# Three of seven products of an Up job keep adding in a bank that another product has filled, and each weight tile is fetched by itself

## The chip, the core and the metric

The kernel runs on one core of a Trainium2 chip. Its engines work side by side: TensorE multiplies matrices and leaves the result in PSUM banks, VectorE and ScalarE work element by element, GpSimd has little to do here, and SyncE issues DMA transfers. Each engine takes its instructions in order. The metric is the time of the whole program in microseconds of the device: median 3076.38 us of 3 runs (3075.09 to 3080.23).

## What is computed

A trunk of two layers over 16 learned tokens and a sequence of 1024, 1040 tokens of width 1024 in float32. Layer 0 mixes tokens by a gated delta rule, layer 1 by an mLSTM. Each is followed by the same MLP, which is where the change lies:

```
def squared_relu_mlp(h, w_up, w_down):
    a = jax.nn.relu(h @ w_up)
    return (a * a) @ w_down

for layer in range(2):
    h = h + mixer(rms_norm(h, attn_norm[layer]))
    h = h + squared_relu_mlp(rms_norm(h, ffn_norm[layer]), ff_up[layer], ff_down[layer])
```

`w_up` is 1024 x 4096, `w_down` 4096 x 1024.

## The kernel before

Everything that is multiplied is split into a high and a low part, and one product is three matmuls (`mm3`, lines 115 to 118): high by high, high by low, low by high.

**Up.** `Up` (line 1025) multiplies by a Strassen-Winograd scheme of two by two blocks: seven products of half size stand for eight. A job is one pair of 128-column strips of `w_up`; there are 16 pairs. Its two weight tiles are r1 (`wraw`, a ring of two buffers) and r2 (one buffer), 512 KB each, which `load` fetches together. `operand` makes the seven weight operands from them: up to four subtractions of 128x512 on VectorE (line 1055), and for each operand a cast on ScalarE (the high part, line 1071) and a subtraction on VectorE (the low part, line 1072). An operand is made three products ahead of its use, in one of four buffers.

The tokens are taken in two halves. A product is twelve matmuls of 128x260 a half (128x256 in layer 1, which leaves the learned tokens out). A job for one half has seven products of twelve matmuls, a job for both has seven of twenty-four. Each layer runs 21 jobs: three for the first half only, while `Norm.combine` (in the background) still makes the operands xhi and xlo of the second half on VectorE and ScalarE; then eleven for both halves, with five one-half jobs between them; and two for one half at the end, at the first of which `first_done` begins to load and split the activation tiles a_st for `Down`.

**Evacuation.** A product's sum stands in one of three PSUM buffers of two banks (`pu`), taken in turn, so a product can begin when the one three before it has been read. `evac` (line 1075) builds the four results with running sums: u is a copy of a11's product (ScalarE), c = u + a12, u = u + s2, v = u + s3, c = v + s1, u = u + s1, c = v + a22, c = u + s4. Those are seven VectorE additions a job. Each c then passes relu and square on ScalarE and goes to the tensor `acts` (d_a) in DRAM.

The program's text gives what depends on what; a scheduler then fixes the order on each engine from its own estimate of times.

Of the kernel before, what the change touches and what calls it, by code (L numbers as in the profile page):

```python
# [7 lines left out]
F32 = mybir.dt.float32  # L8
F32R = mybir.dt.float32r
AF = mybir.ActivationFunctionType  # L10
ALU = mybir.AluOpType
AX = mybir.AxisListType
PSUM = bass.MemoryType.PSUM
DRAM = bass.MemoryType.DRAM

P = 128
D = 1024
KT = D // P
# [37 lines left out]
class Ctx:  # L56
    def __init__(self, tc, stack):
        self.tc = tc
        self.nc = tc.nc
        self.stack = stack  # L60
        self.bg = []
        self.wx = None
# [49 lines left out]

def mm3(nc, ps, whi, wlo, xhi, xlo, first, last):
    nc.tensor.matmul(ps, whi, xhi, start=first, stop=False)  # L116
    nc.tensor.matmul(ps, whi, xlo, start=False, stop=False)  # L117
    nc.tensor.matmul(ps, wlo, xhi, start=False, stop=last)  # L118


def staging(c, shape):
    n = 1
    for d in shape[1:]:
        n *= d
    raw = c.wraw.tile([P, 2 * HALF], F32, tag="wraw", name="wraw")[:, :n]
    return raw.rearrange("p (a b) -> p a b", a=shape[1]) if len(shape) == 3 else raw
# [13 lines left out]
def rows_view(w):  # L140
    return w.rearrange("(k p) f -> p k f", p=P)
# [63 lines left out]
class GDN:  # L205
# [239 lines left out]
    def dense(self, whl, hf, g, m=P):  # L445
        c, n = self.c, GL[hf] // 2
        ps = c.pj.tile([P, 512], F32, tag="pj", name="ps_in")[:m, :n]
        gs = slice(g * n, (g + 1) * n)
        for k in range(KT):
            xhi, xlo = self.xh[k // 2]  # L450
            mm3(self.nc, ps, whl[0][:, k], whl[1][:, k], xhi[:, k % 2, gs], xlo[:, k % 2, gs], k == 0, k == KT - 1)
            if k == KT // 2 - 1:
                yield
        return ps, gs
# [391 lines left out]
class OutUnits:  # L846
# [20 lines left out]
    def unit(self, hf, k8, add, before=None):  # L867
        c, nc = self.c, self.nc
        x = self.pre
        at = self.order.index((hf, k8))  # L870
        w0 = self.load_w(k8, 0)
        x += [self.heads(hf, 4 * k8 + j, at == 3) for j in range(len(x), 4)]
        self.pre = []
        for d in range(KT):
            if before:
                before(d)
            whi, wlo = self.load_w(k8, d) if d else w0
            for g in range(2):
                gs = slice(g * G, (g + 1) * G)
                ps = c.pj.tile([P, 512], F32, tag="pj", name="ps_out")[:, :G]  # L880
                for h in range(8):
                    hi, lo = (t[:, h % 2, gs] for t in x[h // 2])
                    mm3(nc, ps, whi[:, h], wlo[:, h], hi, lo, h == 0, h == 7)
                    if h % 4 == 3:
                        yield
                add(d, g, ps)
            if d == 5 and at < 3:
                nhf, nk8 = self.order[at + 1]
                self.pre = [self.heads(nhf, 4 * nk8 + j, at == 1 and j > 0) for j in range((1, 3, 3)[at])]
# [137 lines left out]
class Up:  # L1027

    ORDER = (("a11", 0), ("a12", 1), ("s2", 4), ("s3", 5), ("s1", 3), ("a22", 6), ("s4", 2))

    def __init__(self, c, w_up, norm, acts, stack, side):
        self.c, self.nc, self.w, self.norm, self.acts = c, c.nc, w_up, norm, acts
        self.u1 = c.pool("u1", 1, stack, side=side)
        self.u3 = c.pool("u3", 3, stack, side=side)
        self.ps = c.pool("pu", 3, stack, space=PSUM)
        self.nop = 0

    def load(self, i):  # L1040
        nc, c, w = self.nc, self.c, rows_view(self.w)
        r1 = staging(c, [P, KT, P])
        nc.sync.dma_start(out=r1, in_=w[:, :, 2 * i * P:(2 * i + 1) * P])
        r2 = self.u1.tile([P, KT, P], F32, tag="r2", name="r2")
        nc.sync.dma_start(out=r2, in_=w[:, :, (2 * i + 1) * P:(2 * i + 2) * P])
        return r1, r2

    def operand(self, raw, name):

# [25 lines left out]
    def evac(self, i, hs, name, ps, tmp):  # L1075

        nc = self.nc

        def tile(pool, n):
            return pool.tile([P, 2, self.norm.g], F32, tag=n, name="up_" + n)[:, hs]  # L1080

        def add(out, x):
            nc.vector.tensor_tensor(out, x, ps, op=ALU.add)  # L1083

        def finish(s, t, x):
            out = tile(self.u3, "c")
            add(out, x)
            nc.scalar.activation(out, out, AF.Relu)
            nc.scalar.activation(out, out, AF.Square)
            nc.scalar.dma_start(out=self.acts[i][:, s, hs, t], in_=out)  # L1090
        if name == "a11":
            tmp["u"] = tile(self.u1, "u")
            nc.scalar.copy(tmp["u"], ps)
        elif name == "a12":
            finish(0, 0, tmp["u"])
        elif name == "s2":
            add(tmp["u"], tmp["u"])
        elif name == "s3":
            tmp["v"] = tile(self.u1, "v")
            add(tmp["v"], tmp["u"])  # L1100
        elif name == "s1":
            finish(1, 1, tmp["v"])
            add(tmp["u"], tmp["u"])
        elif name == "a22":
            finish(1, 0, tmp["v"])
        else:
            finish(0, 1, tmp["u"])

    def run(self, jobs):

        n, ahead = len(self.ORDER), 3
        raws, ops = {0: list(self.load(jobs[0][0]))}, {}
        done = 0
        for ji, (i, parts, before) in enumerate(jobs):
            if before:
                before()
            hs = slice(parts[0], parts[-1] + 1)
            tmp = {}
            for u, (name, xi) in enumerate(self.ORDER):
                while done <= min(ji * n + u + ahead, len(jobs) * n - 1):  # L1120
                    dj, du = divmod(done, n)
                    ops[done] = self.operand(raws[dj], self.ORDER[du][0])
                    if du == n - 1 and dj + 1 < len(jobs):
                        raws[dj + 1] = list(self.load(jobs[dj + 1][0]))
                    done += 1
                w = ops.pop(ji * n + u)
                ps = self.ps.tile([P, 2, 512], F32, tag="pu", name="ps_up")[:, :, :self.norm.g]
                for hf in parts:
                    for k in range(4):
                        hi, lo = (x[:, xi] for x in self.norm.x[hf][k])  # L1130
                        mm3(self.nc, ps[:, hf], w[:, k], w[:, 4 + k], hi, lo, k == 0, k == 3)
                    yield
                self.evac(i, hs, name, ps[:, hs], tmp)

# [599 lines left out]
```

## Time and profile before

| | us |
|---|---|
| median of 3 runs | 3076.38 (3075.09 to 3080.23) |
| profiled execution, device time | 3077.17 |
| its span, first to last instruction | 3075.5 |
| TensorE busy | 3002.4 (98%) |
| VectorE busy | 1934.5 (63%) |
| ScalarE busy | 1473.1 (48%) |
| Up of layer 0 in the span | about 1163 to 1522 |
| Up of layer 1 in the span | about 2369 to 2706 |

Busy times are sums over one profiled execution. "Idle before" names how long an engine stood before an instruction and what released it. The granted clock is TensorE's, in parts of its full 2.4 GHz; 0.5 is the lower of its two levels, 1.2 GHz. A matmul's duration is modelled from its start to its end in a pipeline, so the time of a row of matmuls is read from their starts.

### The profile page before, as it was taken

The numbers are of one execution on the slowest core, as the hardware profiler recorded it, in microseconds if no ns is written. First come the engines' busy times: TensorE is split into PE (matmuls) and PEld (weight loads), VectorE is DVE, ScalarE is ACT, GpSimd is POOL, SyncE is SP. The second block draws the span as 40 slices with busy tenths as digits, with TensorE's granted clock in tenths as the row PEclk, the third lists the DMA queues.
The fourth block names the chain that finished last, engine by engine and source line by source line (L and its number), as shares of the span: only waits on it lengthen the run. The fifth ranks groups of instructions, "written<-read, shape, count | busy, mean of one in ns | idle before, by whom it ended". The sixth has DMA issues, their size and how long they took to land.

```text
span 3075.5 us, 63578 instructions
## 1 busy us (share of the span) xinstructions
PE 3002.4 (98%) x25836; PEld 2848.9 (93%) x25836; DVE 1934.5 (63%) x4393; ACT 1473.1 (48%) x3358; POOL 301.8 (10%) x534
## 2 busy tenths in 40 slices
PE   7999999999999998999999999999999899999999
PEld 7999999999999897999999999999998899988887
DVE  6867777777776568775644547234468876654443
ACT  5666766766664445555411114444444565531112
POOL 1333332232221000000000000000000000000000
PEclk9999999999999999999999999999999999999999
DMA  4333233333234733443423312222132443342223
GB/s 108 82 84 91 83 88 95 86 89 100 81 91 146 237 110 93 138 125 105 155 76 98 104 63 80 66 65 63 61 95 85 122 127 114 115 149 79 93 89 103
DMA packets 401892, 310.22 MB, mean 101 GB/s; under 512 B 29855, under 2 KB 366112, under 8 KB 401600
## 3 DMA queue, kind: packets, MB, share of 16 engines
q1 hardware_dynamic: 366000, 272.32, 30.2%
q10 hardware_dynamic: 35600, 33.84, 3.2%
q8 instruction: 204, 3.34, 0.5%
q14 instruction: 88, 0.72, 0.1%
HBM read 247.79 MB, written 58.31 MB: 100 GB/s over the span
## 4 chain that ended last, share of the span: by engine, by line
PE 84%; DVE 8%; DMA 4%; ACT 2%; POOL 1%; issue 1%; SPq 0%; DVEq 0%; ACTq 0%; POOLq 0%
PE ps_dn L118 8%; PE ps_dn L117 8%; PE ps_dn L116 8%; PE ps_up L116 6%; PE ps_up L117 6%; PE ps_up L118 6%; PE ps_in L118 5%; PE ps_in L116 5%; PE ps_in L117 5%; PE ps_m L116 3%; PE ps_m L117 3%; PE ps_m L118 3%; PE ps_out L116 2%; PE ps_out L117 2%; PE ps_out L118 2%
## 5 line engine op out<-in xcount | busy, mean ns | idle before, releaser
L116 PE MATMUL ps_up<-xhi,uop 128*128 128x260 f32 (+1 forms) x1792 | 509.1, 285 | 21.6 <-DVE up_u L1083 7.1
L118 PE MATMUL ps_up<-xhi,uop 128*128 128x260 f32 (+1 forms) x1792 | 506.5, 283 | 5.1 <-DVE uop L1072 5.1
L117 PE MATMUL ps_up<-xlo,uop 128*128 128x260 f32 (+1 forms) x1792 | 507.6, 283 | 0.7 <-DVE xlo L1020 0.7
L135 ACT CAST whi<-wraw 128x1024 fp32r<-128x1024 f32 (+1 forms) x248 | 255.8, 1032 | 503.8 <-PE ps_dn L117 359.9
L118 PE MATMUL ps_dn<-act_hi,wlo 128*128 128x260 f32 (+1 forms) x1536 | 492.8, 321 | 0.0
L117 PE MATMUL ps_dn<-act_lo,whi 128*128 128x260 f32 (+1 forms) x1536 | 492.3, 320 | 0.0
L116 PE MATMUL ps_dn<-act_hi,whi 128*128 128x260 f32 (+1 forms) x1536 | 490.4, 319 | 0.8 <-DVE up_c L1083 0.7
L116 PE MATMUL ps_in<-act_hi,whi 128*128 128x264 f32 (+1 forms) x1536 | 451.6, 294 | 2.6 <-ACT sz L526 1.7
L118 PE MATMUL ps_in<-act_hi,wlo 128*128 128x264 f32 (+1 forms) x1536 | 448.8, 292 | 0.0
L117 PE MATMUL ps_in<-act_lo,whi 128*128 128x264 f32 (+1 forms) x1536 | 446.6, 291 | 0.0
L136 DVE TENSOR_TENSOR wlo<-wraw,whi 128x1024 fp32r<-128x1024 f32 (+1 forms) x248 | 299.8, 1209 | 167.6 <-ACT whi L135 166.4
L1180 DVE TENSOR_TENSOR hT<-hT,ps_dn 128x260 f32<-128x260 f32 (+1 forms) x384 | 194.9, 510 | 326.1 <-PE ps_dn L118 325.7
L116 PEld LDWEIGHTS ps_up<-xhi,uop 128*128 128x128 f32 x1792 | 340.5, 190 | 26.9 <-ACT uop L1071 8.9
L118 PEld LDWEIGHTS ps_up<-xhi,uop 128*128 128x128 f32 x1792 | 339.8, 190 | 6.4 <-DVE uop L1072 6.4
L117 PEld LDWEIGHTS ps_up<-xlo,uop 128*128 128x128 f32 x1792 | 340.4, 190 | 1.2 <-DVE xlo L1020 1.2
L117 PEld LDWEIGHTS ps_dn<-act_lo,whi 128*128 128x128 f32 x1536 | 288.7, 188 | 24.4
L116 PEld LDWEIGHTS ps_dn<-act_hi,whi 128*128 128x128 f32 x1536 | 288.8, 188 | 23.9 <-DVE up_c L1083 0.9
L118 PEld LDWEIGHTS ps_dn<-act_hi,wlo 128*128 128x128 f32 x1536 | 289.4, 188 | 21.7
L116 PEld LDWEIGHTS ps_in<-act_hi,whi 128*128 128x128 f32 x1536 | 291.2, 190 | 6.5 <-ACT sz L526 2.2
L118 PEld LDWEIGHTS ps_in<-act_hi,wlo 128*128 128x128 f32 x1536 | 290.8, 189 | 3.4 <-issue 1.3
L117 PEld LDWEIGHTS ps_in<-act_lo,whi 128*128 128x128 f32 x1536 | 291.3, 190 | 2.2 <-issue 0.4
L116 PE MATMUL ps_m<-act_hi,whi 128*128 128x260 f32 (+1 forms) x768 | 223.6, 292 | 2.4 <-ACT mso L1447 2.4
(404 smaller groups left out, 6424.6 us busy)
## 6 DMA issues: line engine op xcount, KB each, us to landing
wraw<-in_gdn_in_dram SPq DMA_DIRECT2D x96, 512.0 KB, 4.0
wraw<-in_ff_down_dram SPq DMA_DIRECT2D x72, 512.0 KB, 3.4
wraw<-in_ff_up_dram SPq DMA_DIRECT2D x42, 512.0 KB, 4.8
r<-in_ff_up_dram SPq DMA_DIRECT2D x42, 512.0 KB, 4.5
a_st<-d_a SPq DMA_DIRECT2D x32, 520.0 KB, 3.7
wraw<-in_gdn_out_dram SPq DMA_DIRECT2D x32, 512.0 KB, 4.0
a_st<-d_a SPq DMA_DIRECT2D x32, 512.0 KB, 5.2
wraw<-in_mlstm_in_dram SPq DMA_DIRECT2D x28, 512.0 KB, 3.8
```

What stands on the lines that cost most here:

```text
L116: nc.tensor.matmul(ps, whi, xhi, start=first, stop=False)
L117: nc.tensor.matmul(ps, whi, xlo, start=False, stop=False)
L118: nc.tensor.matmul(ps, wlo, xhi, start=False, stop=last)
L135: nc.scalar.copy(hi, raw)
L136: nc.vector.tensor_tensor(lo, raw, hi.bitcast(F32), op=ALU.subtract)
L1180: nc.vector.tensor_tensor(hT[:, d, t0:t0 + n], hT[:, d, t0:t0 + n], ps, op=ALU.add)
```

## The change

The products of a job come in another order (a11, s2, s3, a12, s1, a22, s4) and use three buffers with names of their own, A, B and C. a11, s2, s3 and s1 start a sum afresh (A, B, C, B). a12, a22 and s4 go on adding to what stands in their buffer (A, C, B), after it has been read. So c for a12 is complete in the buffer, and ScalarE's relu reads it from there; c for a22 is u plus buffer C (s3 and a22), c for s4 is u plus buffer B (s1 and s4). Five VectorE additions a job are left. The two weight tiles of the next job are fetched one by one: r1 after the third operand (s3) has been made, r2 after the sixth (a22).

```diff
+def mm3(nc, ps, whi, wlo, xhi, xlo, first, last, more=False):
+    nc.tensor.matmul(ps, whi, xhi, start=first and not more, stop=False, skip_group_check=more)
+    nc.tensor.matmul(ps, whi, xlo, start=False, stop=False, skip_group_check=more)
+    nc.tensor.matmul(ps, wlo, xhi, start=False, stop=last, skip_group_check=more)
...
-    ORDER = (("a11", 0), ("a12", 1), ("s2", 4), ("s3", 5), ("s1", 3), ("a22", 6), ("s4", 2))
+    ORDER = (("a11", 0, "A", True), ("s2", 4, "B", True), ("s3", 5, "C", True), ("a12", 1, "A", False),
+             ("s1", 3, "B", True), ("a22", 6, "C", False), ("s4", 2, "B", False))
...
-        self.ps = c.pool("pu", 3, stack, space=PSUM)
+        self.ps = c.pool("pu", 1, stack, space=PSUM)
...
-    def load(self, i):
-        nc, c, w = self.nc, self.c, rows_view(self.w)
-        r1 = staging(c, [P, KT, P])
-        nc.sync.dma_start(out=r1, in_=w[:, :, 2 * i * P:(2 * i + 1) * P])
-        r2 = self.u1.tile([P, KT, P], F32, tag="r2", name="r2")
-        nc.sync.dma_start(out=r2, in_=w[:, :, (2 * i + 1) * P:(2 * i + 2) * P])
-        return r1, r2
+    def load(self, i, second):
+        w = rows_view(self.w)
+        r = self.u1.tile([P, KT, P], F32, tag="r2", name="r2") if second else staging(self.c, [P, KT, P])
+        f0 = (2 * i + second) * P
+        self.nc.sync.dma_start(out=r, in_=w[:, :, f0:f0 + P])
+        return r
...
         def finish(s, t, x):
             out = tile(self.u3, "c")
-            add(out, x)
-            nc.scalar.activation(out, out, AF.Relu)
+            if x is None:
+                nc.scalar.activation(out, ps, AF.Relu)
+            else:
+                add(out, x)
+                nc.scalar.activation(out, out, AF.Relu)
...
-        elif name == "a12":
-            finish(0, 0, tmp["u"])
...
+        elif name == "a12":
+            finish(0, 0, None)
         elif name == "s1":
             finish(1, 1, tmp["v"])
-            add(tmp["u"], tmp["u"])
         elif name == "a22":
-            finish(1, 0, tmp["v"])
+            finish(1, 0, tmp["u"])
...
-                    if du == n - 1 and dj + 1 < len(jobs):
-                        raws[dj + 1] = list(self.load(jobs[dj + 1][0]))
+                    if dj + 1 < len(jobs) and du in (2, 5):
+                        raws.setdefault(dj + 1, []).append(self.load(jobs[dj + 1][0], du == 5))
...
-                ps = self.ps.tile([P, 2, 512], F32, tag="pu", name="ps_up")[:, :, :self.norm.g]
+                if first:
+                    banks[bank] = self.ps.tile([P, 2, 512], F32, tag="pu" + bank, name="ps_up")[:, :, :self.norm.g]
+                ps = banks[bank]
```

How this moves instructions is shown at three places. The first is VectorE in layer 0, where the first two-half job (the fourth, "job 3" when counted from 0) begins; wraw and r2 are the two weight tiles, s3 an operand made from both, uop an operand, up_u and up_v the running sums, st_b, st_t and xlo belong to the second half's token operands. Before:

```order
L1017 TENSOR_TENSOR st_t_17081<-st_b_17080,st_t_17081 128x260
L1083 TENSOR_TENSOR up_c_17369<-up_u_17338,ps_up_17344 128x520
L1072 TENSOR_TENSOR uop_17341<-r2_17226,uop_17341 128x512
L1072 TENSOR_TENSOR uop_17374<-r2_17226,uop_17374 128x512
L1022 TENSOR_TENSOR xlo_17083<-st_t_17081,xhi_17082 128x1040
L1055 TENSOR_TENSOR s3_17505<-wraw_17407,r2_17409 128x512
L1055 TENSOR_TENSOR r2_17409<-r2_17409 128x512
L1083 TENSOR_TENSOR up_u_17338<-up_u_17338,ps_up_17377 128x520
L1072 TENSOR_TENSOR uop_17404<-wraw_17224,uop_17404 128x512
L1072 TENSOR_TENSOR uop_17438<-wraw_17407,uop_17438 128x512
```

After, at the first sums of the same job:

```order
L1056 TENSOR_TENSOR wraw_17136<-wraw_17136 128x512
L1073 TENSOR_TENSOR uop_17390<-wraw_17136,uop_17390 128x512
L1084 TENSOR_TENSOR up_u_17325<-up_u_17325,ps_up_17331 128x520
L1073 TENSOR_TENSOR uop_17357<-r2_17194,uop_17357 128x512
L1084 TENSOR_TENSOR up_v_17387<-up_u_17325,ps_up_17362 128x520
L1073 TENSOR_TENSOR uop_17421<-wraw_17278,uop_17421 128x512
L1056 TENSOR_TENSOR s3_17454<-wraw_17278,r2_17360 128x512
L1056 TENSOR_TENSOR wraw_17278<-r2_17360,s3_17454 128x512
L1056 TENSOR_TENSOR r2_17360<-r2_17360 128x512
L1084 TENSOR_TENSOR up_c_17449<-up_v_17387,ps_up_17424 128x520
```

Before, the sum into u (up_u_17338) stands behind s3_17505, which needs the tile r2_17409 of the next job. After, the sums into u and v of job 3 stand ahead of the s3 that needs the next tile r2_17360, and job 3's c for a12 is gone from VectorE; the token operands have been finished earlier.

The second place is SyncE's queue at the start of layer 0's Up, where the weight tiles of the first jobs are fetched. Before:

```order
L1043 DMA wraw_16778<-in_ff_up_dram 128x8x128
L1043 DMA wraw_16866<-in_ff_up_dram 128x8x128
L1045 DMA r2_16780<-in_ff_up_dram 128x8x128
L1045 DMA r2_16868<-in_ff_up_dram 128x8x128
L1043 DMA wraw_17063<-in_ff_up_dram 128x8x128
L1045 DMA r2_17065<-in_ff_up_dram 128x8x128
L1043 DMA wraw_17224<-in_ff_up_dram 128x8x128
L1045 DMA r2_17226<-in_ff_up_dram 128x8x128
```

After:

```order
L1046 DMA wraw_16778<-in_ff_up_dram 128x8x128
L1046 DMA wraw_16794<-in_ff_up_dram 128x8x128
L1046 DMA r2_16780<-in_ff_up_dram 128x8x128
L1046 DMA wraw_16952<-in_ff_up_dram 128x8x128
L1046 DMA r2_16835<-in_ff_up_dram 128x8x128
L1046 DMA r2_17034<-in_ff_up_dram 128x8x128
L1046 DMA wraw_17136<-in_ff_up_dram 128x8x128
L1046 DMA wraw_17278<-in_ff_up_dram 128x8x128
L1046 DMA r2_17194<-in_ff_up_dram 128x8x128
```

Before, a tile r1 (wraw) and a tile r2 alternate. After, r1 runs ahead: wraw_17278 of the fifth job stands ahead of r2_17194 of the fourth (r2_17360, the fifth's, comes two fetches later).

The third place is ScalarE near the end of layer 0's Up, in the last but one job, where act_hi is the high part of an activation tile of Down and a_st its landing buffer. Before:

```order
L1089 ACTIVATE up_c_20735<-up_c_20735 128x260
L1071 CAST uop_20764<-s3_20740 128x512
L1159 CAST act_hi_20908<-a_st_20615 128x1040
L1090 DMA d_a0_14_78<-up_c_20735 128x260
L1071 CAST uop_20743<-wraw_20678 128x512
```

After:

```order
L1092 ACTIVATE up_c_20639<-up_c_20639 128x260
L1093 ACTIVATE up_c_20639<-up_c_20639 128x260
L1164 CAST act_hi_20803<-a_st_20522 128x1040
L1094 DMA d_a0_14_78<-up_c_20639 128x260
L1072 CAST uop_20644<-s3_20621 128x512
L1092 ACTIVATE up_c_20659<-up_c_20659 128x260
L1097 COPY up_u_20680<-ps_up_20667 128x260
```

The cast of the last job's operand s3 stood ahead of the cast of act_hi, and now stands behind it.

## Rows read from the trace of the kernel before

**Rows 1.** The page, busy time of each engine, share of the span and instructions
```profile
PE 3002.4 (98%) x25836; PEld 2848.9 (93%) x25836; DVE 1934.5 (63%) x4393; ACT 1473.1 (48%) x3358; POOL 301.8 (10%) x534
```

**Rows 2.** Stretches through both Up stages: busy time by engine, clock, DMA share, GB/s
```profile
1163.00:1230.00 67.00, 54.42 (x423) 51.98 (x421) 58.61 (x111) 37.27 (x72) 0.00 (x0) 0.97 0.31 91
1231.00:1300.00 69.00, 69.00 (x566) 69.00 (x565) 49.92 (x84) 38.33 (x71) 0.00 (x0) 0.98 0.46 139
1300.00:1480.00 180.00, 180.00 (x1509) 180.00 (x1508) 114.55 (x185) 96.06 (x167) 0.00 (x0) 1.00 0.38 114
1500.00:1512.00 12.00, 8.13 (x45) 7.41 (x44) 10.13 (x16) 5.90 (x12) 0.00 (x0) 0.72 0.67 214
1512.00:1522.00 10.00, 8.69 (x69) 8.13 (x68) 7.56 (x12) 7.36 (x13) 0.76 (x5) 1.00 0.82 271
2369.00:2428.00 59.00, 49.91 (x374) 46.26 (x374) 55.14 (x107) 35.63 (x72) 0.00 (x0) 0.97 0.32 94
2500.00:2690.00 190.00, 190.00 (x1601) 190.00 (x1601) 124.27 (x200) 102.47 (x178) 0.00 (x0) 1.00 0.39 117
2690.00:2706.00 16.00, 13.67 (x108) 12.95 (x107) 13.76 (x27) 10.99 (x23) 0.00 (x0) 1.00 0.69 223
```

**Rows 3.** TensorE's waits over the span: us in total, times, longest us
```profile
PE ps_up L116 <- DVE up_u L1083: 7.1, 7, 2.2
PE ps_up L116 <- ACT uop L1071: 5.1, 4, 1.9
PE ps_up L118 <- DVE uop L1072: 5.1, 5, 1.8
PE ps_up L116 <- DVE up_c L1083: 3.2, 4, 1.3
```

**Rows 4.** TensorE's timeline in layer 0: start us, us, line, operation [idle before <-releaser]
```profile
1228.44 0.28 PE L118 MATMUL ps_up<-xhi,uop 128*128 128x260 f32 x1
1230.70 0.39 PE L116 MATMUL ps_up<-xhi,uop 128*128 128x260 f32 x1 [1.98 <-DVE up_u L1083]
```

**Rows 5.** VectorE's timeline in layer 0, waits for the second weight tile
```profile
1180.37 0.69 DVE L1055 TENSOR_TENSOR s<-wraw,r 128x512 f32<-128x512 f32 x1 [1.12 <-DMA r<-in_ff_up_dram]
...
1228.62 0.69 DVE L1055 TENSOR_TENSOR s<-wraw,r 128x512 f32<-128x512 f32 x1 [3.04 <-DMA r<-in_ff_up_dram]
1229.34 0.69 DVE L1055 TENSOR_TENSOR r<-r 128x512 f32<-128x512 f32 x1
1229.95 0.69 DVE L1083 TENSOR_TENSOR up_u<-up_u,ps_up 128x520 f32<-128x520 f32 x1
```

**Rows 6.** A stretch of 3 us behind the wait at 1230.70
```profile
1231.00:1234.00 3.00, 3.00 (x18) 3.00 (x17) 3.00 (x6) 0.00 (x0) 0.00 (x0) 0.57 0.42 116
```

**Rows 7.** VectorE's timeline, instructions back to back
```profile
1210.33 0.68 DVE L1072 TENSOR_TENSOR uop<-wraw,uop 128x512 fp32r<-128x512 f32 x1
1210.93 0.96 DVE L1020 TENSOR_TENSOR xlo<-st_b,xhi 128x780 fp32r<-128x780 f32 x1
1211.82 0.42 DVE L1083 TENSOR_TENSOR up_c<-up_v,ps_up 128x260 f32<-128x260 f32 x1
1212.15 0.42 DVE L1083 TENSOR_TENSOR up_u<-up_u,ps_up 128x260 f32<-128x260 f32 x1
```

**Rows 8.** VectorE's groups by shape: count | busy, mean ns | idle before
```profile
L1012 DVE SCALAR_TENSOR_TENSOR st_b<-hT,ncols,nr 128x520 f32<-128x520 f32 x16 | 11.4, 754 | 0.1
L1022 DVE TENSOR_TENSOR xlo<-st_t,xhi 128x1040 fp32r<-128x1040 f32 x8 | 9.9, 1235 | 0.5 <-ACT xhi L1021 0.5
```

**Rows 9.** TensorE's timeline at the end of layer 0's Up
```profile
1520.89 0.39 PE L116 MATMUL ps_dn<-act_hi,whi 128*128 128x260 f32 x1 [0.66 <-DVE up_c L1083]
```

**Rows 10.** The page, DMA issues: count, KB each, median us from issue to landing
```profile
a_st<-d_a SPq DMA_DIRECT2D x32, 520.0 KB, 3.7
```

**Rows 11.** VectorE's timeline in a one-half job of the middle
```profile
1302.88 0.42 DVE L1083 TENSOR_TENSOR up_u<-up_u,ps_up 128x260 f32<-128x260 f32 x1
1304.33 0.43 DVE L1083 TENSOR_TENSOR up_v<-up_u,ps_up 128x260 f32<-128x260 f32 x1
```

More of the change, by code (lines that the diff above doesn't have):

```diff
@@ L110, in step @@
             gens.remove(g)
[L115 to L118, printed above, removed]
+def mm3(nc, ps, whi, wlo, xhi, xlo, first, last, more=False):
+    nc.tensor.matmul(ps, whi, xhi, start=first and not more, stop=False, skip_group_check=more)
+    nc.tensor.matmul(ps, whi, xlo, start=False, stop=False, skip_group_check=more)
+    nc.tensor.matmul(ps, wlo, xhi, start=False, stop=last, skip_group_check=more)
 def staging(c, shape):
@@ L1111, in run @@
         n, ahead = len(self.ORDER), 3
-        raws, ops = {0: list(self.load(jobs[0][0]))}, {}
+        raws, ops = {0: [self.load(jobs[0][0], j) for j in range(2)]}, {}
         done = 0
@@ L1117, in run @@
             hs = slice(parts[0], parts[-1] + 1)
-            tmp = {}
-            for u, (name, xi) in enumerate(self.ORDER):
+            tmp, banks = {}, {}
+            for u, (name, xi, bank, first) in enumerate(self.ORDER):
                 while done <= min(ji * n + u + ahead, len(jobs) * n - 1):
@@ L1130, in run @@
                         hi, lo = (x[:, xi] for x in self.norm.x[hf][k])
-                        mm3(self.nc, ps[:, hf], w[:, k], w[:, 4 + k], hi, lo, k == 0, k == 3)
+                        mm3(self.nc, ps[:, hf], w[:, k], w[:, 4 + k], hi, lo, k == 0, k == 3, not first)
                     yield
```

## The prediction

> **What bounds the kernel now.** I read the engine totals first. TensorE is busy 3002.4 of 3075.5 us [rows 1], so the change can return only what lies in its holes, and only those of the Up stages. Next came the table of stretches through both Up stages [rows 2]. In the steady middle TensorE never stops: 1509 matmuls in 180 us are 0.1193 us each, or 1.43 us for a product of twelve, while VectorE works 114.55 us. Nothing can be gained there. At the two starts VectorE is the pace: it works 58.61 of 67 us (layer 0) and 55.14 of 59 us (layer 1).
>
> What TensorE loses in a stretch is its length less its matmuls at 0.1193 us:
> - layer 0, start: 67 − 423 × 0.1193 = 16.5 us, and 69 − 566 × 0.1193 = 1.5 us behind it;
> - layer 0, end: 12 − 45 × 0.1193 = 6.6 us and 10 − 69 × 0.1193 = 1.8 us, together 8.4 us;
> - layer 1, start: 59 − 374 × 0.1193 = 14.4 us; end: 16 − 108 × 0.1193 = 3.1 us.
>
> That is 44 us, the most that any change of Up could give back. The list of waits says who ends them [rows 3]: VectorE's sum into u (7.1 us) and into c (3.2 us), the cast of a weight operand (5.1 us) and the subtraction that makes its low half (5.1 us). So it is about half evacuation and half operands.
>
> The largest single hole shows how they mix. TensorE's 1228.44 row is followed by the one at 1230.70, which waited for u [rows 4]. On VectorE that sum stands behind two operand subtractions, and the first of them sat idle for 3.04 us for the second weight tile to arrive [rows 5]. Behind the hole come slow matmuls: 18 in 3 us at a granted clock of 0.57, where 25 fit at full speed; that is 3 − 18 × 0.1193 = 0.85 us in this window and about 1.5 us until full speed [rows 6].
>
> **The change, part by part.** *Fewer sums.* Seven VectorE sums a job become five: a12's product comes out whole in bank A, and the sum of s1 into u is done by the bank. Over 42 jobs that is 84 instructions. Back to back, a 128x260 sum starts 0.33 to 0.335 us after the one before it [rows 7]. Only those at the starts and ends count, since in the middle VectorE has room. A start holds three one-half jobs, so six sums or 2.0 us; an end two jobs, so four or 1.35 us.
>
> *The order of the starts.* Removing sums is not the whole of it, since the order moves too, so I added up VectorE's work that must precede the matmul that waits longest, and subtracted TensorE's own work up to there. Back to back costs: 128x512 0.605, 128x780 0.88, any 128x260 addition (Up's sums, and those that make Up's token operands) 0.335 [rows 7]; the statistics step and the 1040-wide subtraction 0.67 and 1.155, their durations less the 0.08 by which neighbours overlap [rows 8]. Counts are from the instruction order.
> - Layer 0 before, at matmul 317: 39 × 0.605 + 34 × 0.335 + 8 × 0.67 + 4 × 0.88 + 3 × 1.155 + 0.4 = 47.7 us, less 317 × 0.1193 = 37.8, so TensorE is 9.9 us behind. At job 3's u (matmul 372) it is still 9.4; with VectorE's idle waits for weights, 3.04 + 1.12 [rows 5], 13.6, and with the slow matmuls 15.1. The stretches gave 16.5 + 1.5, so the method is right to 3 us.
> - Layer 0 after: the scheduler draws the second half's operands further forward. The worst place is now job 2's v, at matmul 230: 32 × 0.605 + 26 × 0.335 + 5.4 + 3.5 + 3.5 + 0.4 = 40.8 us, less 27.4 = 13.4 us. The wait ahead of job 3's u is gone, but the second weight tile still can't be fetched before a22's operand is made, and is needed one product earlier; I put 2.1 us of idle VectorE for that, half-way between nothing and the 4.2 us of before. Sum 15.5: no gain, ± 2.5.
> - Layer 1 by the same count, at matmul 317 before and 316 after: the instructions ahead are the same kinds, with 64 128x256 additions before and 58 after, so 6 × 0.335 = 2.0 us less work; with a little for the wait ahead of job 3's u, −2.5 ± 1.5.
>
> *The ends.* The four sums are worth 1.35 us where they stand on the path. Also the last sum waits less for its buffer: TensorE's wait at 1520.89 (0.66 us) ends on that c [rows 9]. Against it, ScalarE's cast of the last s3 operand now stands behind the cast of a Down tile, which waits for its load, 3.7 us from issue to landing in the median [rows 10]. Between +3.7 and −4 I take −1.5 ± 3 in layer 0, −0.5 ± 1.5 in layer 1.
>
> *Bank reuse.* Before, three buffers turn, so a product waits for the sum of the one three earlier. Now s1 opens the bank of s2 with only a12 between, and the next s2 that of s4. In a two-half job the cover is 2.86 us. In a one-half job it is 1.43 us: the sums of successive products start 1.45 us apart, the products' own pace, and last 0.42 us [rows 11], so about 1.0 us is left in the middle, and I cost it at nothing there. The bounds are 0 and 0.5 us at two places in each of the ten one-half jobs in the middle, +10 us at the worst; the value nearest to the row is 0. At the starts VectorE's queue is full, and the worst place above already holds that wait.
>
> *Loads.* As many bytes, issued apart; and DMA is busy 0.38 of the middle [rows 2]: nothing there; a second tile that is late in a one-half job falls under rival 3. *ScalarE's* relu reads a12 from the bank instead of from c; were that 0.1 us dearer, it works 96.06 of 180 us [rows 2] and hides it. Nothing.
>
> Sum: 0 − 2.5 − 1.5 − 0.5 = −4.5 us, with an own range of ± 4.5. The profiled execution took 3077.17 us (span 3075.5 and 1.7 around it), 0.8 above the median of 3076.38. So 3077.2 − 4.5 = 3072.7, or 3072 against the median.
>
> **A rule against it.** The clock was 1.00 through 180 us in which three buffers of two banks turned without a pause [rows 2], and 0.57 behind the hole at 1230.70 [rows 6]. The Trainium skill ("TensorE: Matmul & The Clock Gate", section "A second HAM failure mode: psum-queue depth-cycling") reports a kernel whose cycling through PSUM banks made TensorE pause often enough for the clock to swing. By that rule tighter reuse of the banks would bring slow stretches into the middle; by the row, turning the banks alone brings none, only a hole does. It stands behind the second half of rival 3.
>
> **The rivals.**
> 1. *Full relief.* If job 3's hole goes in layer 0 with its slow matmuls (2.1 + 1.5) and nothing takes its place, both starts gain their six sums (4.0), the ends their four (2.7), and half of VectorE's 4.2 us of weight waits goes (2.1): −12.4, so 3064. For it: u is the largest waiter [rows 3]. Against: the work count of layer 0, which finds the same lag elsewhere.
> 2. *Nothing.* The starts are paced by the operands (in layer 0's count 23.6 of 47.7 us are 128x512 subtractions, and 21 sums are 7.0), the order puts the six sums' time into waits for weights in layer 1 as in layer 0, and the gain at the ends is eaten by the load: 0 ± 2, so 3076. For it: the casts and subtractions end 10.2 us of waits, no fewer than the sums [rows 3].
> 3. *Slower, by bank reuse.* The place is s1 behind u's sum and s2 behind the last sum of the job, in one-half jobs. It decides when a sum starts more than 1.0 us after its product. If each of the ten middle jobs pauses 0.3 us twice, +6; at the end the cast behind the load adds 2 and its slow matmuls 1.5; less the 2.5 of layer 1: +7, so 3083. For it: VectorE is 58.61 of 67 us busy where one-half jobs stand. Against: in the middle each sum comes at its product's pace [rows 11], so none queues behind another.
> 4. *The change isn't what it seems:* sums leave VectorE, but TensorE adds the same matmuls. It adds none: a continued bank changes flags only, 5376 matmuls before and after. Chance near nothing.
>
> **How the numbers follow.** A measurement of this kernel can tell 0.2%, 6 us, from no change: faster is under 3070.2, slower over 3082.5. Forecast 0.49, of which 0.36 of it under 3070.2; rival 1 0.21, nearly all faster; rival 2 0.17, all same; rival 3 0.13, of it 0.10 slower. Faster 0.38, same 0.51, slower 0.11. The range leaves a tenth on each side: half of rival 1 below 3064.5, and rival 3 above 3080.
>
> **What would show it.** Right: sums of Up on VectorE fall from 294 to 210 and ScalarE reads a12 from the bank; the hole at job 3's u disappears, but a wait for v or u of job 2 appears in layer 0's first 50 us, and TensorE loses 15 to 18 us there; in layer 1's start it loses 11 to 13. The middle stays at 0.1193 us a matmul and a clock of 1.00. Wrong: waits for u or c in one-half jobs of the middle (rival 3), or a start of layer 0 that loses under 12 us (rival 1); a layer-0 end that loses over 11 us would show the cast behind the load.

## The result and the profile after

The changed kernel takes 3112.61 us (median of 4 runs, 3104.84 to 3113.52), the kernel before 3078.31 in the same runs: a ratio of 1.0107 [1.0092, 1.0123], some 34 us slower, outside the predicted range. The profiled execution is the shortest of the four, 3104.84 us with a span of 3102.8; so the trace shows 27.3 of the 34 us [rows 1 for the engines before].

The page of the changed kernel, busy time by engine:

```profile
PE 3018.0 (97%) x25836; PEld 2859.5 (92%) x25836; DVE 1895.1 (61%) x4309; ACT 1463.0 (47%) x3358; POOL 301.6 (10%) x534
```

VectorE has the 84 instructions less (4393 to 4309) that were forecast, and 39 us less work. TensorE issues as many matmuls as before, yet is busy 15.6 us longer: part of its matmuls ran slow.

The stretches of both Up stages in the changed kernel (length, busy time of PE, PEld, DVE, ACT and POOL with counts, granted clock, DMA share, GB/s):

```profile
1158.00:1240.00 82.00, 70.10 (x525) 67.94 (x524) 66.17 (x119) 44.81 (x88) 0.00 (x0) 0.92 0.31 91
1240.00:1480.00 240.00, 237.07 (x1953) 234.41 (x1952) 138.90 (x223) 120.33 (x223) 0.00 (x0) 1.00 0.39 118
1500.00:1520.00 20.00, 15.30 (x101) 13.71 (x101) 16.82 (x26) 13.45 (x25) 0.58 (x5) 0.91 0.80 237
2369.00:2430.00 61.00, 53.09 (x385) 49.36 (x386) 54.70 (x101) 35.06 (x73) 0.00 (x0) 0.94 0.29 84
2430.00:2600.00 170.00, 159.79 (x1258) 157.03 (x1257) 96.17 (x160) 81.76 (x160) 0.00 (x0) 0.95 0.39 120
2700.00:2728.00 28.00, 24.38 (x179) 23.52 (x179) 19.54 (x32) 18.25 (x33) 0.00 (x0) 0.88 0.53 170
2552.50:2556.50 4.00, 3.97 (x20) 3.76 (x20) 2.65 (x5) 1.50 (x4) 0.00 (x0) 0.57 0.10 33
```

Two stretches of the kernel before, the steady middles, for comparison:

```profile
1240.00:1480.00 240.00, 240.00 (x2011) 240.00 (x2009) 157.33 (x257) 130.01 (x231) 0.00 (x0) 1.00 0.40 122
2430.00:2600.00 170.00, 170.00 (x1436) 170.00 (x1435) 119.92 (x202) 95.99 (x179) 0.00 (x0) 1.00 0.43 130
```

What TensorE lost is again the length less the count at 0.1193 us (layer 1: 0.1187, the pace of its middle in [rows 2]). The starts hardly moved: 82 − 525 × 0.1193 = 19.4 us against 19.0, and 61 − 385 × 0.1187 = 15.3 against 14.4. (The prediction has 18.0 for layer 0's start; its two stretches leave out the microsecond from 1230 to 1231, and the whole from 1163 to 1300 gives 137 − 989 × 0.1193 = 19.0.) The ends: 8.0 against 8.4, and 6.8 against 3.1. But the middles, which lost nothing before, lose 240 − 1953 × 0.1193 = 7.0 us in layer 0 and 170 − 1258 × 0.1187 = 20.7 us in layer 1. In these stretches Up loses 32 us more. From its first matmul to its last, Up takes 361.1 us in layer 0 (before 353.1) and 365.9 in layer 1 (339.3), so 34.6 us more in all; the work ahead of the first Up and between the two took 7 us less in this execution.

TensorE's waits in the changed kernel (us in total, times, longest us), to be read against [rows 3]:

```profile
PE ps_up L117 <- ACT uop L1072: 22.7, 14, 3.6
PE ps_up L117 <- DVE up_c L1084: 7.5, 12, 1.1
PE ps_up L119 <- DVE uop L1073: 6.6, 5, 2.6
PE ps_up L117 <- DVE up_v L1084: 0.9, 2, 0.5
PE ps_up L117 <- DVE up_u L1084: 0.5, 1, 0.5
```

The wait for u went from 7.1 to 0.5 us, as the order had said. In its place stands the cast of an operand, 22.7 us against 5.1, and c, 7.5 against 3.2.

One hole of layer 1's middle shows how. It is the end of a one-half job. First SyncE's queue, the fetches of the two weight tiles:

```profile
2542.08 0.37 SPq L1046 DMA_DIRECT2D wraw<-in_ff_up_dram  x1
2543.01 0.37 SPq L1046 DMA_DIRECT2D r<-in_ff_up_dram  x1
```

Then VectorE: the last use of the old r1 (the first row, the low part of s4's operand), the last use of the old r2 (the second row, that of a22's), the operands of the next job, and the last sum of this one:

```profile
2541.36 0.69 DVE L1073 TENSOR_TENSOR uop<-wraw,uop 128x512 fp32r<-128x512 f32 x1 [0.17 <-ACT uop L1072]
...
2542.30 0.68 DVE L1073 TENSOR_TENSOR uop<-r,uop 128x512 fp32r<-128x512 f32 x1
...
2549.78 0.69 DVE L1056 TENSOR_TENSOR s<-wraw,r 128x512 f32<-128x512 f32 x1 [4.35 <-DMA r<-in_ff_up_dram]
2550.51 0.69 DVE L1056 TENSOR_TENSOR wraw<-r,s 128x512 f32<-128x512 f32 x1
2551.12 0.68 DVE L1056 TENSOR_TENSOR r<-r 128x512 f32<-128x512 f32 x1
2551.72 0.41 DVE L1084 TENSOR_TENSOR up_c<-up_u,ps_up 128x256 f32<-128x256 f32 x1
```

ScalarE's cast of the next s3:

```profile
2550.57 0.62 ACT L1072 CAST uop<-s 128x512 fp32r<-128x512 f32 x1 [4.23 <-DVE s L1056]
```

And TensorE:

```profile
2551.24 0.39 PE L117 MATMUL ps_up<-xhi,uop 128*128 128x256 f32 x1 [1.97 <-ACT uop L1072]
...
2552.28 0.36 PE L117 MATMUL ps_up<-xhi,uop 128*128 128x256 f32 x1 [0.54 <-DVE up_c L1084]
```

Read from the top. r1 of the job after next is issued 0.93 us ahead of r2 of the next job. r2 is issued the moment its buffer is free (the row at 2542.30 ends at 2542.98), and is used 6.8 us later. VectorE stands idle for 4.35 us in front of the subtraction that needs it, and everything behind it in its queue stands too: s4's sum starts at 2551.72, behind that subtraction and two more. ScalarE's cast waits for the first subtraction, TensorE 1.97 us for that cast and then 0.54 us for s4's sum, whose bank the next s2 opens. The stretch behind the holes has a granted clock of 0.57: 20 matmuls in 4 us where 33 fit (the last of the stretches above).

In the kernel before, r2 and r1 come the other way round at such a place, in a one-half job of layer 1's middle. SyncE, and VectorE's subtraction:

```profile
2526.90 0.37 SPq L1045 DMA_DIRECT2D r<-in_ff_up_dram  x1
2528.34 0.37 SPq L1043 DMA_DIRECT2D wraw<-in_ff_up_dram  x1
```

```profile
2531.47 0.69 DVE L1055 TENSOR_TENSOR s<-wraw,r 128x512 f32<-128x512 f32 x1 [0.87 <-DMA r<-in_ff_up_dram]
```

r1 is issued 1.44 us behind r2, r2 is used 4.57 us after its issue, and VectorE stands 0.87 us for it. Over the span VectorE sat idle for r2 79.6 us in the changed kernel, against 58.8 before. Its group of that subtraction in the changed kernel (count, busy us, mean ns, idle before it and its releaser), and in the kernel before:

```profile
L1056 DVE TENSOR_TENSOR s<-wraw,r 128x512 f32<-128x512 f32 x42 | 29.0, 691 | 79.6 <-DMA r<-in_ff_up_dram 79.6
```

```profile
L1055 DVE TENSOR_TENSOR s<-wraw,r 128x512 f32<-128x512 f32 x42 | 29.0, 691 | 58.8 <-DMA r<-in_ff_up_dram 58.8
```

### The profile page after: what moved, and what is told of

It is laid out like the page before. It is cut to its first block, busy times and chain, and to the rows that moved or that the text cites. A ratio compares the mean times of both kernels' runs of the same rounds, so it can differ in the third digit from the quotient of the medians.

```text
span 3102.8 us, 63390 instructions
## 1 busy us (share of the span) xinstructions
PE 3018.0 (97%) x25836; PEld 2859.5 (92%) x25836; DVE 1895.1 (61%) x4309; ACT 1463.0 (47%) x3358; POOL 301.6 (10%) x534
## 4 chain that ended last, share of the span: by engine, by line
PE 44%; DVE 3%; DMA 2%; ACT 1%; issue 1%; ACTq 0%; DVEq 0%; SPq 0%
PE ps_dn L119 8%; PE ps_dn L118 8%; PE ps_dn L117 8%; PE ps_m L117 3%; PE ps_m L118 3%; PE ps_m L119 3%; PE ps_up L117 2%; PE ps_up L119 2%; PE ps_up L118 2%; DMA r<-in_ff_up_dram 2%; PE ps_mo L117 1%; PE ps_mo L119 1%; PE ps_mo L118 1%; DVE uop L1073 1%; PE mpc L1530 1%
## 5 line engine op out<-in xcount | busy, mean ns | idle before, releaser
L117 PE MATMUL ps_up<-xhi,uop 128*128 128x260 f32 (+1 forms) x1792 | 516.8, 289 | 34.0 <-ACT uop L1072 22.7
L119 PE MATMUL ps_up<-xhi,uop 128*128 128x260 f32 (+1 forms) x1792 | 510.9, 288 | 7.0 <-DVE uop L1073 6.6
L117 PEld LDWEIGHTS ps_up<-xhi,uop 128*128 128x128 f32 x1792 | 345.9, 193 | 43.7 <-ACT uop L1072 35.5
L119 PEld LDWEIGHTS ps_up<-xhi,uop 128*128 128x128 f32 x1792 | 344.7, 193 | 10.7 <-DVE uop L1073 10.4
L118 PEld LDWEIGHTS ps_up<-xlo,uop 128*128 128x128 f32 x1792 | 346.3, 193 | 0.4 <-DVE xlo L1021 0.3
L117 PEld LDWEIGHTS ps_dn<-act_hi,whi 128*128 128x128 f32 x1536 | 288.8, 188 | 22.7
```

Source lines behind the costliest of these rows:

```text
L117: nc.tensor.matmul(ps, whi, xhi, start=first and not more, stop=False, skip_group_check=more)
L118: nc.tensor.matmul(ps, whi, xlo, start=False, stop=False, skip_group_check=more)
L119: nc.tensor.matmul(ps, wlo, xhi, start=False, stop=last, skip_group_check=more)
```

## The experiments

Each ratio is to executions of the kernel before that were measured together with it, with its 95% interval.

| kernel | us | ratio |
|---|---|---|
| changed | 3112.61 | 1.0107 [1.0092, 1.0123] |
| together_fetch | 3111.55 | 1.0118 [1.0101, 1.0135] |
| r1_behind | 3086.90 | 1.0041 [1.0026, 1.0056] |
| r2_once | 3068.29 | 0.9977 [0.9964, 0.9989] |
| r2_halves | 3063.78 | 0.9960 [0.9949, 0.9971] |
| r2_sooner | 3096.56 | 1.0065 [1.0050, 1.0080] |
| loads_alone | 3075.50 | 1.0003 [0.9991, 1.0015] |
| order_alone | 3095.12 | 1.0060 [1.0044, 1.0076] |
| order_own_u | 3085.04 | 1.0037 [1.0024, 1.0051] |
| order_r2_once | 3083.10 | 1.0013 [0.9999, 1.0026] |
| order_own_u_r2_once | 3075.38 | 1.0003 [0.9993, 1.0012] |
| banks_old_order | 3091.73 | 1.0049 [1.0034, 1.0064] |
| banks_halves | 3083.06 | 1.0011 [1.0001, 1.0021] |
| before_r2_once | 3066.44 | 0.9966 [0.9954, 0.9977] |
| before_halves | 3064.02 | 0.9949 [0.9936, 0.9961] |
| one_square_buffer | 3077.17 | 1.0000 [0.9985, 1.0014] |

**Is it r2? r2_once.** The changed kernel with

```diff
+        if second and self.r2 is not None:
+            return self.r2
         r = self.u1.tile([P, KT, P], F32, tag="r2", name="r2") if second else staging(self.c, [P, KT, P])
+        if second:
+            self.r2 = r
```

Two theories stand against each other here. O: the new order asks for r2 one product earlier than its only buffer lets it arrive. K: a bank is opened again with only one product in between, and TensorE waits for the sum that reads it.

> The changed kernel, but r2 is fetched once a layer and read by all 21 jobs, so no operand waits for its transfer; products, sums and operands are as many as in the changed kernel, the results of all jobs but the first use the wrong second tile. Theory O: 3060 to 3074 us, the waits for an operand of ScalarE (22.7 us in the changed kernel) under 6, and the waits for c in one-half jobs (7.5 us) mostly gone, since s4's sum no longer queues behind a subtraction that waits for r2. Theory K: 3095 to 3112 us, the waits for c remain.

```profile
PE ps_up L117 <- ACT uop L1076: 5.6, 6, 1.6
PE ps_up L117 <- DVE up_c L1088: 2.3, 3, 1.5
```

These are TensorE's waits in it for an operand's cast and for c. 3068.29 us, as theory O had it: with order, banks and sums unchanged, taking away r2's transfer takes away the whole loss. The waits for an operand's cast fall from 22.7 to 5.6 us, those for c from 7.5 to 2.3. Theory K fell as the cause of this kernel's loss.

**What makes r2 late? r1_behind and together_fetch.** In the first, a copy of one element a row makes r1's fetch wait until the r2 before it has landed:

```diff
+        if behind is not None:
+            self.nc.gpsimd.tensor_copy(r[:, 0, 0:1], behind[:, 4, 0:1])
...
-raws.setdefault(dj + 1, []).append(self.load(jobs[dj + 1][0], du == 5))
+raws.setdefault(dj + 1, []).append(self.load(jobs[dj + 1][0], du == 5, raws[dj][1] if du == 2 else None))
```

> The changed kernel, but each r1 is held until the r2 issued before it has landed: GpSimd copies one element a row of that r2 into r1's buffer before r1 is fetched over it. Order, banks and sums as in the changed kernel. Theory Q (in the changed kernel r1 of the job after next stands 0.93 or 2.75 us ahead of r2 of the next job in SyncE's queue, and shares the DMA engines with it, so that r2 is used 5.0 to 6.9 us after its issue where 4.1 is had when r1 isn't ahead): the middles lose under 8 us together where they lost 29, 3080 to 3095 us. Theory S (only the lost product of slack counts, whatever is ahead): 3103 to 3116 us.

3086.90 us. The stretches of its middles, and one r2 with its use:

```profile
1240.00:1480.00 240.00, 239.28 (x1997) 238.87 (x1996) 142.16 (x230) 122.97 (x229) 9.33 (x14) 1.00 0.40 120
2430.00:2600.00 170.00, 167.59 (x1399) 166.42 (x1398) 103.94 (x174) 88.36 (x174) 7.18 (x11) 1.00 0.42 127
```

```profile
2547.98 0.37 SPq L1048 DMA_DIRECT2D r<-in_ff_up_dram  x1
```

```profile
2551.99 0.69 DVE L1058 TENSOR_TENSOR s<-wraw,r 128x512 f32<-128x512 f32 x1 [2.84 <-DMA r<-in_ff_up_dram]
```

The middles lose 1.8 and 170 − 1399 × 0.1187 = 3.9 us, 22 us less than in the changed kernel, and r2 is used 4.0 us after its issue. That r1 goes ahead is thus shown to be the larger part. It isn't all: two r2 of layer 1's middle are still used 5.9 and 6.0 us after their issue here, with no r1 near them, and the kernel stays 0.41% above the one before; beside the middles the trace has some 5 us more lost at starts and ends, most of it at layer 1's end. The second puts both fetches back behind s4's operand:

```diff
-                    if dj + 1 < len(jobs) and du in (2, 5):
-                        raws.setdefault(dj + 1, []).append(self.load(jobs[dj + 1][0], du == 5))
+                    if dj + 1 < len(jobs) and du == n - 1:
+                        raws[dj + 1] = [self.load(jobs[dj + 1][0], j) for j in range(2)]
```

> The changed kernel with both weight tiles fetched together behind s4's operand, as before; order, banks and sums as changed. If the order and the banks put r1 ahead (s4's operand, r1's last reader, is made before a22's, r2's last reader), r1 stays ahead of r2 in the middle and the loss stays, 3098 to 3116 us. If the separate fetches do, the loss goes as in r1_behind, 3080 to 3092 us.

3111.55 us: nothing changed. The same place on SyncE and VectorE:

```profile
2548.11 0.37 SPq L1046 DMA_DIRECT2D wraw<-in_ff_up_dram  x1
2549.04 0.37 SPq L1046 DMA_DIRECT2D r<-in_ff_up_dram  x1
```

```profile
2555.87 0.69 DVE L1056 TENSOR_TENSOR s<-wraw,r 128x512 f32<-128x512 f32 x1 [4.41 <-DMA r<-in_ff_up_dram]
```

r1 is again 0.93 us ahead, and r2 is used 6.8 us after its issue. So the separate fetches are not at fault. r1's buffer comes free with s4's operand and r2's with a22's, and the fetches go in the order in which their buffers come free. In the program's text a22's operand is made ahead of s4's, in both kernels. The scheduler has turned that round in the changed kernel, as VectorE's rows at 2541.36 and 2542.30 show, and it runs s3's product ahead of s2's. In order_alone, order_own_u and banks_old_order r2 stays ahead of r1 through both middles: neither the order nor the banks alone puts r1 ahead. Why the scheduler turns it round in the whole change isn't shown.

**The fetches alone.** loads_alone is the kernel before with the changed `load` and the rule `du in (2, 5)`, nothing else.

> The kernel before with the new fetches alone: r1 after the third operand, r2 after the sixth; order, banks and sums as before. In SyncE's queue r1 and r2 still alternate here, r2 of a job ahead of r1 of the next. Theory Q: no loss, 3070 to 3082 us. A rival that puts the loss on the fetches by themselves: 3088 us or more.

No change, as theory Q said.

**The order alone.** order_alone has only the new `ORDER`, with a11's copy kept in c's ring; order_own_u gives it a buffer of its own:

```diff
-    ORDER = (("a11", 0), ("a12", 1), ("s2", 4), ("s3", 5), ("s1", 3), ("a22", 6), ("s4", 2))
+    ORDER = (("a11", 0), ("s2", 4), ("s3", 5), ("a12", 1), ("s1", 3), ("a22", 6), ("s4", 2))
...
-            tmp["u"] = tile(self.u1, "u")
-            nc.scalar.copy(tmp["u"], ps)
+            tmp["w"] = tile(self.u1, "w")
+            nc.scalar.copy(tmp["w"], ps)
```

> The kernel before with the new order of the seven products alone: three rotating buffers, seven sums a job and both tiles fetched together as before (a11 is copied into the buffer of c, where a12's sum is added later). Theory O (the order asks for the second weight tile r2 one product earlier than its only buffer lets it arrive): the loss stays, 3100 to 3115 us, with VectorE idle on r2 for some 75 us over the span as in the changed kernel (79.6) against 58.8 before. Theory K (a bank is reused with one product between): the loss goes, 3072 to 3082 us.

> The new order alone as in order_alone, but a11's copy has a buffer of its own instead of one of the ring of c (one buffer of squares for the room). If the order costs by r2's slack, the ratio to the kernel before stays at 1.003 to 1.006. If order_alone's loss was the ring of c, it is 0.999 to 1.001.

> order_alone (3095.12 us) with r2 fetched once a layer and read by all jobs (the results of all jobs but the first use the wrong second tile). If the order costs only by the product of slack that it takes from r2, this falls to 3062 to 3072 us, where r2_once (3068.29) and before_r2_once (3066.44) are. If the order of the starts costs by itself, it stays at 3080 us or more.

> order_own_u with r2 fetched once a layer (the results of all jobs but the first use the wrong second tile). If the order costs only through r2, the ratio to the kernel before is that of before_r2_once, 0.996 to 0.998. If the order of the starts costs by itself, 1.000 or more.

order_alone, at 3095.12 us, missed both of its ranges, and VectorE's idle time for r2 is 39.0 us in it, not some 75: less than the 58.8 of the kernel before. So idle time for r2 is no measure of the loss, and theory O in that form fell for the order alone. 1.0060 and 1.0037: some of order_alone's loss may have been the ring of c (the intervals overlap), but the order costs by itself. Not in the middles, where r1 stays behind r2 (stretches of order_own_u):

```profile
1240.00:1480.00 240.00, 240.00 (x2005) 240.00 (x2005) 158.91 (x255) 127.27 (x226) 0.00 (x0) 1.00 0.39 120
2430.00:2600.00 170.00, 170.00 (x1432) 170.00 (x1431) 120.33 (x199) 95.40 (x176) 0.00 (x0) 1.00 0.42 128
```

What it costs lies at the starts and ends, then, where one-half jobs follow each other and the next s2 comes 1.43 us sooner. This trace shows only part of it: it is the shortest of six executions, 3075.94 us, and from its first matmul to its last Up takes 5 us longer in it than before, all in layer 1 (344.7 us against 339.3). Its waits:

```profile
PE ps_up L116 <- ACT uop L1071: 15.2, 9, 3.1
PE ps_up L116 <- DVE up_u L1083: 5.8, 4, 2.3
```

15.2 us for a cast against 5.1 in [rows 3]. With r2 fetched once that falls to 7.1, and the ratio to 1.0003. But before_r2_once is at 0.9966, so I had it wrong that the order costs through r2: 0.37% remain against it, as many as with r2 fetched for every job; order_r2_once (3083.10 us) stays above 3080 too. The profiled execution of order_own_u_r2_once is the shortest of its twelve. From first to last matmul Up takes 346.3 and 342.3 us in it, against 344.7 and 338.7 in before_r2_once, so 5 of these 11 us show; which wait makes them wasn't settled.

**The banks in the old order.** banks_old_order lets a22 go on in s3's buffer and s4 in s1's, in the order of before:

```diff
+    ORDER = (("a11", 0, "A", True), ("a12", 1, "B", True), ("s2", 4, "A", True), ("s3", 5, "C", True),
+             ("s1", 3, "B", True), ("a22", 6, "C", False), ("s4", 2, "B", False))
```

> The order and the loads of before; buffers with names, in which a22 goes on adding to s3 and s4 to s1, so six sums a job instead of seven; s2 opens a11's buffer with a12 between, the next a12 that of s4 with a11 between. Theory O: no loss, 3068 to 3080 us, the middle at 0.1193 us a matmul. Theory K: a loss of 0.5 us and a slow stretch of 1.5 us at one or two places of each one-half job, 3090 to 3110 us.

> banks_old_order (3091.73 us) with r2 in half tiles as in r2_halves. If a bank that is reused with one product between costs only where its sum queues on VectorE behind a subtraction that waits for r2, this falls to 3060 to 3070 us and the middle loses nothing. If the reuse costs by itself, it stays at 3078 us or more, with waits for c in the middle.

1.0049, and with r2 early 1.0011 where before_halves is at 0.9949. Here the banks do cost by themselves, against theory O. The middles of banks_halves, and one hole:

```profile
1240.00:1480.00 240.00, 236.95 (x1971) 236.05 (x1971) 153.11 (x240) 126.02 (x225) 0.00 (x0) 1.00 0.40 120
2430.00:2600.00 170.00, 166.77 (x1391) 165.49 (x1391) 113.69 (x184) 92.75 (x173) 0.00 (x0) 1.00 0.41 125
```

```profile
1309.51 0.28 PE L118 MATMUL ps_up<-xhi,uop 128*128 128x260 f32 x1
1310.40 0.36 PE L116 MATMUL ps_up<-xhi,uop 128*128 128x260 f32 x1 [0.61 <-DVE up_c L1085]
```

They lose 4.9 us each, most of it 0.77 us at each of ten one-half jobs (five in either middle), because the scheduler put s4 directly ahead of the a12 that opens s4's bank. r2_sooner moves a12 behind a22 (`a11, s2, s3, s1, a22, a12, s4`) and shows the same with s1 and u:

> The changed kernel with a12 moved behind a22 (a11, s2, s3, s1, a22, a12, s4), and r2 fetched after the fifth operand: r2's last reader is made one product sooner, so the next s3 has four products again, as before. s1 now opens s2's buffer with only s3 between. Theory O: most of the loss goes, 3070 to 3088 us. Theory K: no gain, 3100 to 3118 us, with waits for u in one-half jobs.

```profile
1296.71 0.28 PE L119 MATMUL ps_up<-xhi,uop 128*128 128x260 f32 x1
1297.59 0.36 PE L117 MATMUL ps_up<-xhi,uop 128*128 128x260 f32 x1 [0.61 <-DVE up_u L1084]
```

```profile
1297.02 0.43 DVE L1084 TENSOR_TENSOR up_u<-up_u,ps_up 128x260 f32<-128x260 f32 x1 [1.25 <-PE ps_up L119]
```

The sum starts 0.31 us after the product's last matmul, takes 0.43, and TensorE goes on 0.14 us after it. So a bank that is opened at once costs 0.76 us even if its sum queues behind nothing. The middles of r2_sooner lose 4.7 and 6.4 us, and the starts and ends more than before; 3096.56 us misses theory O's 3070 to 3088 and lies just under theory K's 3100, with the waits for u that K named. In the instruction order of these two kernels no matmul stands between, at one place of every one-half job of the middle. In those of the changed kernel and of r2_halves below it is 11 matmuls or more, about a product, and with r2 in time that is enough.

**r2 in time, for good.** r2_halves is the changed kernel with r2 in two half tiles and a ring of three:

```diff
-        r = self.u1.tile([P, KT, P], F32, tag="r2", name="r2") if second else ...
+        r = [self.u3.tile([P, KT // 2, P], F32, tag="r2", name="r2") for _ in range(2)]
+        for h in range(2):
+            self.nc.sync.dma_start(out=r[h], in_=w[:, 4 * h:4 * h + 4, f0:f0 + P])
...
-name="nsq", bufs=2)
+name="nsq", bufs=1)
```

> The changed kernel with r2 as two half tiles (a21, a22) in a ring of three buffers, so that a21 of the next job is fetched at any time and a22 when s1's operand has been made; the buffer of squares in Norm goes from two to one for the room. Theory O: the next s3 is never late in the middle, 3062 to 3078 us. If bank reuse or the order of the starts is what counts, 3090 us or more.

before_halves does the same to the kernel before, and one_square_buffer is the control of the last line.

> The kernel before (its order, three rotating buffers, seven sums a job, fetches together) with r2 in half tiles in a ring of three and one buffer of squares, as in r2_halves (3063.78 us). If the 12 us that r2_halves gains over the kernel before come of r2's earlier fetch, this gains as much, 3060 to 3069 us, and order, banks and sums are worth nothing. If the sums and the order gave them, it stays at 3072 to 3080 us.

> The kernel before, but r2 is fetched once a layer and read by all jobs (the results of all jobs but the first use the wrong second tile): the control of r2_once (3068.29 us). If the eight us that r2_once is under the kernel before come of the sums, this stays at 3073 to 3080 us. If they come of no longer waiting for r2, it falls to 3064 to 3071 us.

> The kernel before with one buffer of squares instead of two, the control for the room that the half tiles took. Every theory: no change, 3070 to 3081 us.

One buffer of squares changes nothing. r2_halves and before_halves beat the kernel before by 0.40% and 0.51%, 12 and 16 us, and before_r2_once (3066.44 us) falls as far as r2_once. The middles of r2_halves, and VectorE's idle time for r2 in it and in before_halves (after the bar: busy us, mean ns, idle us):

```profile
1230.00:1480.00 250.00, 250.00 (x2092) 250.00 (x2091) 152.08 (x240) 132.00 (x240) 0.00 (x0) 1.00 0.40 122
2420.00:2590.00 170.00, 170.00 (x1434) 170.00 (x1434) 108.49 (x176) 91.47 (x176) 0.00 (x0) 1.00 0.43 129
```

```profile
L1061 DVE TENSOR_TENSOR s<-wraw,r 128x512 f32<-128x512 f32 x42 | 29.0, 690 | 2.4 <-DMA r<-in_ff_up_dram 1.2
```

```profile
L1056 DVE TENSOR_TENSOR s<-wraw,r 128x512 f32<-128x512 f32 x42 | 29.0, 690 | 1.1
```

Nothing is lost in the middles, and the idle time before that subtraction, 79.6 us in the changed kernel, is 2.4 and 1.1. Since both kernels land at 3064 us, and r2_once and before_r2_once within 0.11%, the banks, the order and the 84 sums together are worth nothing that these runs show. Their parts don't add up singly: the order alone costs 0.37%, the banks in the old order 0.5 to 0.6%. No run takes the sums alone away, so what they give back of that isn't shown.

## Why the prediction was wrong

- **The view of the bound was right, and the middle was left out of it.** Up's holes were the only thing to gain from, and VectorE paced the starts. But "Nothing can be gained there", said of the middles, hid that something could be lost there, and 28 of the 32 us were.
- **The step that failed is the one on loads**: "nothing there; a second tile that is late in a one-half job falls under rival 3". It was priced by the share of the DMA engines, 0.38, not by the queue. The instruction order had it: in the rows of SyncE ahead of the prediction r1 of the fifth job stands ahead of r2 of the fourth. I read that as a matter of the start; the trace shows the same through the middle. What it costs, 5.0 to 6.9 us from issue to use where the one-half jobs of the middle before had 4.4 to 4.7, was in no row before, but could have been bounded by an estimate: one more 512 KB transfer ahead of it (4.8 us from issue to landing for r1 in the page of before). The product of slack that the new order takes from r2 was priced at layer 0's start alone, at 2.1 us. In the middle it costs nothing while r1 is behind (order_own_u); with r1 ahead the two together make r2 late.
- **Bank reuse: cost at nothing, with a bound of 10 us.** As a mechanism it was named rightly, s2 behind the last sum of the job, from the point where a sum starts more than 1.0 us after its product. That point was reached, since the sum queued behind the subtraction that waited for r2. With r2 in time the price of nothing held: r2_halves reuses the banks alike, and its middles lose nothing. Rival 3 so had the place and the sign, and a chance of 0.13; its price of 0.3 us a pause lacked r2's own wait (1.97 us of TensorE's time in the hole above, and 0.54 for the bank) and most of the slow matmuls behind each hole.
- **Layer 0's start, no gain ± 2.5**: right (+0.4), though not by the wait forecast: v of job 2 cost 0.5 us, the operands of the first jobs the rest. **Layer 1's start, −2.5**: +0.9, since the operands waited there too. **The ends, −1.5 and −0.5**: −0.4 and +3.7; the cast behind Down's load, one of its bounds, did show. ScalarE at the end of layer 0's Up:

```profile
1505.42 1.06 ACT L1164 CAST act_hi<-a_st 128x1040 fp32r<-128x1040 f32 x1 [1.85 <-DMA a_st<-d_a]
...
1506.38 0.61 ACT L1072 CAST uop<-s 128x512 fp32r<-128x512 f32 x1
```

```profile
1507.05 0.39 PE L117 MATMUL ps_up<-xhi,uop 128*128 128x260 f32 x1 [3.56 <-ACT uop L1072]
```

  The cast of the last s3 comes behind act_hi, which waited 1.85 us for its load, and TensorE waited 3.56 us for that cast, at 1507.05. The load explains 1.6 of them: VectorE had s3 ready at 1504.81, itself late, since r2 was used 6.25 us after its issue. In layer 0 the rest of the end lost that much less; in layer 1 TensorE waited 2.07 us for the cast of the last s3, there not directly behind a load, and 1.39 for the next, and the end lost 3.7 more.
- **The sums, 2.0 us a start and 1.35 an end**: r2_halves against before_halves puts them, with the order and the banks, at nothing to a loss of 0.1%; alone they were not measured. Rival 2's reason, that operands end no fewer waits than sums, was 10.2 us against 10.3 in its rows, so a tie.
- **The rule on cycling through banks** found no support of its own: in r2_halves the same reuse of three named buffers runs through both middles at a clock of 1.00. In its trace and the changed kernel's, every slow stretch of Up stands behind a hole of 0.5 us or more.

## What to carry to other kernels

Before taking work off an engine that paces a stretch, look at what that engine waits for: here a transfer into a single buffer. Fetching it earlier gave 0.4 to 0.5%, and fewer sums with the order and banks that they need gave nothing on top. When a change reorders who frees buffers, read the DMA queue's order through the steady state too, and the order that the scheduler made, not the text's: here a transfer that nobody needed soon, ahead of the urgent one, put that one off by 0.9 to 2.8 us. A wait in an engine's queue is paid by everything behind it; here a sum that freed a bank stood behind a subtraction that had waited 4.35 us.

## What was not expected of the hardware

A 512 KB transfer that was issued 0.93 us behind another on the same queue was used 5.0 to 5.1 us after its issue at the five such places of layer 0's middle but 6.6 to 6.9 us at four of five in layer 1's, against 3.9 to 4.3 us where, in the same middles, the other was 17 us or more ahead. Both have a DMA share of 0.39. The trace shows one difference: while each of the four late tiles was on its way, the queue that brings instructions moved a packet of 16 KB, begun 3.3 to 3.7 us after the tile's issue, and it moved none while any of the five in layer 0 was. That this is the cause isn't shown: in r1_behind, with such a packet under way, some tiles took 5.9 and 6.0 us and others 4.1. Nor does any trace show where the 8 us come from by which the other executions of the changed kernel are above the profiled one.
